# Moving the weight sums, the sums of squares and the closing normalisation of a hybrid decoder layer

## The chip, the cores and the metric

The program runs on one core of one Trainium2 chip. Its engines work side by side, each through its own queue in order: TensorE (PE in the profile; PEld is its loading of weights), VectorE (DVE), ScalarE (ACT) and GpSimd (POOL) compute; SyncE (SP) starts the transfers (DMA). The metric is device microseconds for one execution, lower is better; the number compared is the median over runs.

## What is computed

One decoder layer over 1024 tokens of width 1024, float32, with three sub-layers. Each is a root-mean-square norm, a function, another norm and an addition to the residual stream:

```
def rmsnorm(x, g):
    xf = x * rsqrt(mean(x * x, axis=-1) + 1e-6)
    return xf * g

h = rmsnorm(x, g_mix_pre)                       # 1 mixing: S5 state space + chunked gMLP
mix = concat([y_ssm(h), y_gmlp(h)]) @ w_out
x = x + rmsnorm(mix, g_mix_post)
h = rmsnorm(x, g_x_pre)                         # 2 cross-attention, 4 heads, 256 memory tokens
q, k, v = h @ w_q, mem_n @ w_k, mem_n @ w_v
x = x + rmsnorm((softmax(q k^T / 16) v) @ w_o, g_x_post)
h = rmsnorm(x, g_ffn_pre)                       # 3 gated convolutional FFN, d_ff 2816
a = causal_conv3(h @ w_up)
x = x + rmsnorm((a_val * gelu(a_gate)) @ w_down, g_ffn_post)
```

## The kernel before

**Layout.** Activations lie transposed: a tile holds 128 channels by 512 tokens. The tokens are two halves, h = 0 and 1, so a full activation is eight tiles per half. To keep float32 precision each operand is split into a high and a low part (a copy on ScalarE, a subtraction on VectorE or GpSimd), and each product is three matmuls (`mm3`, L227). Weights come through a stream (`Stream`, L64): SP loads a 128x512 raw tile, ScalarE makes the high part (L131), VectorE the low part (L134). PSUM has four banks "acc", three "sx" and one "st". The up and down projections use Strassen-like block products, for which sums of weight blocks are formed on GpSimd; for the down projection these are made beforehand by `s_sums` (L1342): for each of 11 blocks four loads, four sums (L1354), four stores to DRAM scratch "sd".

**Order.** The Python program gives a priority, and a scheduler that simulates the engines fixes the order of every queue before the launch. While `self.pinned` is true, the instructions passed through `pin` (L222) keep the program's order. Work beside the main products is written as generators that advance by one `yield` at each tick; `mm3` ticks twice for each product of eight blocks.

**Attention (L1048).** For each half the projection "o1" (L1094: eight products of 24 matmuls) makes the output of the mixers. `post(..., "q", ...)` (L712) then takes the statistics (L715), and for each of eight tiles loads a residual tile "rs" (L722, two buffers), multiplies (L723, VectorE), adds the residual (L724, GpSimd), stores x1d (L725), makes the high and the low part of the query input (L729, L730), squares (L709, ScalarE) and adds the square to a running sum (L710, GpSimd in this mode). The generator then passes `Q_STATS` = 3 ticks and calls `rms` (L738 through L273): matmuls against ones (L278) that sum over channels, and an inverse square root in small VectorE steps (L261 to L270). The result `qscale` enters the softmax as the scale of the exponentials (L1128). In the loop over six stages (L1163) stage i computes the query blocks of head i (`q_block`, two of 24 matmuls), the scores and softmax of head i-1 (`scores`), and the transposes (L1142) and weighted sums of head i-2. A step of `s_sums` is taken at most places of this loop, so it runs through both halves. The output projection "o2" follows; during half 0's the `post` of half 1 runs at its side, and during the attention of half 1 the `post2[0]` of half 0 (mode "f": sums of squares on VectorE). Attention's tiles "t" (11 buffers) hold queries, probabilities and transposes.

**End (L1442).** The last block product accumulates into four banks, first 256 columns of half 1 (quarter 0: 11 blocks by 4 banks by 3 matmuls of 256 columns), then the other 256 (quarter 1). Beside quarter 0 the generator `first_half` (L1497) sums the squares of half 0's eight tiles, and `finish` (L755) takes statistics, broadcasts them (L305, then a copy to SBUF, L308), multiplies (L766) and adds the residual (L767), and stores. In quarter 1 the order is pinned from the second bank on; after block `TAIL_R` = (1, 1) come the statistics of quarter 0, after `TAIL_B` = (1, 9) their broadcast, and its four pairs of tiles are finished (L774, L776) between the matmuls. After quarter 1 the same follows for its own columns.

Of the kernel before, what the change touches and what calls it, by code (L numbers as in the profile page):

```python
# [43 lines left out]
Q_STATS = 3  # L44
TAIL_R = (1, 1)
TAIL_B = (1, 9)
# [9 lines left out]
SLOTS_2 = {"kv": 16, "t": 11, "rs": 2}  # L56
# [95 lines left out]
class Builder:  # L152
# [120 lines left out]
    def rms(self, acc, nt):  # L273

        nc = self.nc
        ps = self.bank("st")
        for i in range(nt):
            self.pin(nc.tensor.matmul(ps[:, i:i + 1], lhsT=acc[:, i * P:(i + 1) * P], rhs=self.ones[:, 0:1],  # L278
                                      start=True, stop=True))
        x = self.tiny([P, nt], "st_x", 2)  # L280
        self.pin(nc.vector.tensor_scalar(x, ps[:, :nt], 1.0 / D, EPS, ALU.mult, ALU.add))
        return self.rsqrt(x, [P, nt])
# [17 lines left out]
    def bcast(self, r, nt, tag="st"):  # L300

        nc = self.nc
        ps = self.bank("st")
        for i in range(nt):
            self.pin(nc.tensor.matmul(ps[:, i * P:(i + 1) * P], lhsT=r[:, i:i + 1].to_broadcast([P, P]),  # L305
                                      rhs=self.ident, start=True, stop=True))
        bc = self.slot(tag)
        nc.scalar.copy(bc[:, :nt * P], ps[:, :nt * P])  # L308
        return ps, bc
# [402 lines left out]
    def post(self, m, acc, gpost, res, h, mode, dst):  # L712
# [5 lines left out]
        outp = self.xg[h] = []  # L718
        for i in range(KT):
            x = m[i]  # L720
            rs = self.slot("rs")
            nc.sync.dma_start(rs, res(i, h))  # L722
# [9 lines left out]
            self.sumsq(x, acc2, i == 0, v if mode == "f" else g)  # L732
            yield
        if mode == "q":
            self.ready[h] = True
            for _ in range(Q_STATS):
                yield
# [17 lines left out]
    def finish(self, m, acc, h, x2d):  # L755

        nc, v, g = self.nc, self.nc.vector, self.nc.gpsimd
        res = []
        for i in range(KT):
            t = self.slot("rs")  # L760
            nc.sync.dma_start(t, x2d[i][h])
            res.append(t)
        r, bc = yield from self.stats(acc, 4)
        for i in range(KT):
            x = m[i]
            v.scalar_tensor_tensor(x, x, self.gain["g_ffn_post"][:, i:i + 1], bc, ALU.mult, ALU.mult)  # L766
            g.tensor_tensor(x, x, res[i], ALU.add)  # L767
            yield
            nc.sync.dma_start(self.out[P * i:P * i + P, HALF * h:HALF * h + HALF], x)
# [33 lines left out]
    def prepare(self, cp, dp):  # L803
# [78 lines left out]
        self.ready = [False, False]  # L882
        self.mix = {}
# [164 lines left out]
    def attention(self):  # L1048
# [41 lines left out]
        post = [None, None]  # L1090
        kv = self.side(kv_parts(), 1)
        for h in range(2):
            for b in range(8):
                proj(lambda k, hh: self.mix[k, hh], "o1", m1, sq1, b, h, (4, 5, 6, 7, 0, 1, 2, 3))  # L1094
            for k in range(8):
# [64 lines left out]
        s_job = self.s_sums()  # L1160
        for h in range(2):
            heads = lambda k, hh: oT[hh][k]
            for i in range(6):  # L1163
# [5 lines left out]
                if i == 1:  # L1169
                    self.drain(post[h])  # L1170
                if 1 <= i <= 4:
                    scores(h, i - 1)
                for j in range(2):
                    if i:
                        next(s_job, None)
                    if i < 4:
                        q_block(h, i, j)
                    if i >= 2:
                        turn(i - 2) if j == 0 else weigh(h, i - 2)
            self.xg[h] = []  # L1180
            if h == 0:
                self.side(post[1])
# [159 lines left out]
    def s_sums(self):  # L1342

        nc, g = self.nc, self.nc.gpsimd
        for k in range(11):
            t = {}
            for o in range(2):
                for j in range(2):
                    t[o, j] = self.slot("m")
# [92 lines left out]
    def down(self):  # L1442
# [74 lines left out]

        for k in range(11):
# [7 lines left out]
            next(job, None)  # L1526
        self.drain(job)
        st = {}
        for b in range(4):
            self.pinned = b > 0  # L1530
            for k in range(11):
                one(k, b, quarters[1])
                if (b, k) == TAIL_R:
                    st["r"] = self.rms(sq[1][:, quarters[0]], 2)
                if (b, k) == TAIL_B:
                    bc = self.bcast(st["r"], 2)[1]
# [87 lines left out]
```

## Time and profile before

| what | us |
|---|---|
| median of 3 runs (1373.46 to 1376.73) | 1373.87 |
| profiled execution, its own time | 1375.64 |
| its span, first to last instruction | 1373.8 |
| VectorE busy in the span | 1066.1 |
| GpSimd busy in the span | 694.6 |
| ScalarE busy in the span | 628.0 |

The difference between the own time and the span lies outside the instructions. Busy time of an engine that is not the bottleneck costs nothing by itself; what matters in each stretch is which wait ended last. Matmuls are pipelined, so one may last 0.4 us in the profile while the next starts 0.23 us after it. A bracket at the end of a timeline line gives the idle time before it and what ended it.

### The profile page before, as it was taken

The page shows a single profiled execution, that of the slowest core. Times are in us where ns is not written, and L with a number is a line of the kernel's source. Part 1 is how long each engine was busy: PE and PEld are TensorE (multiplying, and loading weights), DVE is VectorE, ACT ScalarE, POOL GpSimd, SP SyncE. Part 2 cuts the span into 40 slices and gives each one's busy share as a digit, 9 for nine tenths or more (in the row PEclk, how much of TensorE's full clock was granted, in tenths as well). Part 3 has the DMA queues.
Part 4 walks back from the last instruction along what each step waited for, and adds up shares of the span by engine and source line. Part 5 has one row for each costly group of instructions (what it writes and reads, how often), then busy time and mean ns, then how long its engine had stood idle before and what let it go on. Part 6 is the DMA issues. An engine that isn't in the chain of part 4 may idle for free. (4 is left out here: it accounts for less than half of the span.)

```text
span 1373.8 us, 19246 instructions
## 1 busy us (share of the span) xinstructions
PE 1275.9 (93%) x6352; PEld 1080.4 (79%) x6352; DVE 1066.1 (78%) x1619; ACT 628.0 (46%) x1172; POOL 694.6 (51%) x532
## 2 busy tenths in 40 slices
PE   9799898779998999769999999999999999999993
PEld 7689897678886888558887878888888888788883
DVE  7968799876377757796657978888899879966576
ACT  7223331246444445345544654555555554446340
POOL 1586355834258524860343838656565227822144
PEclk9899999899998999979999999999999999999996
DMA  9654326256348844772358566545454359755123
GB/s 319 185 143 134 93 73 182 85 148 192 93 125 263 299 134 125 266 245 85 83 163 282 161 209 229 180 149 161 146 182 140 107 198 383 233 159 175 56 79 136
DMA packets 150662, 233.58 MB, mean 170 GB/s; under 512 B 33697, under 2 KB 43041, under 8 KB 150561
## 3 DMA queue, kind: packets, MB, share of 16 engines
q1 hardware_dynamic: 150560, 232.34, 53.3%
q8 instruction: 50, 0.82, 0.3%
q14 instruction: 52, 0.42, 0.1%
HBM read 174.23 MB, written 53.85 MB: 166 GB/s over the span
## 5 line engine op out<-in xcount | busy, mean ns | idle before, releaser
L233 PE MATMUL acc<-b,w 128*128 128x512 f32 x2412 | 587.9, 397 | 11.4 <-DVE b L730 4.4
L233 PEld LDWEIGHTS acc<-b,w 128*128 128x128 f32 x2412 | 457.6, 191 | 110.2 <-DVE b L730 6.5
L134 DVE TENSOR_TENSOR w<-raw,w 128x512 fp32r<-128x512 f32 x206 | 203.1, 994 | 94.2 <-PE acc L233 64.6
L233 PE MATMUL sx<-b,w 128*128 128x512 f32 x921 | 222.6, 391 | 1.7 <-ACT T L1277 1.7
L233 PEld LDWEIGHTS sx<-b,w 128*128 128x128 f32 x921 | 174.0, 189 | 38.5 <-ACT T L1277 2.1
L131 ACT CAST w<-raw 128x512 fp32r<-128x512 f32 x228 | 141.4, 622 | 125.3 <-PE acc L233 72.1
L710 POOL TENSOR_TENSOR ac<-ac,sq 128x512 f32<-128x512 f32 x52 | 78.3, 1513 | 153.2 <-ACT sq L709 152.6
L233 PE MATMUL acc<-T,w 128*128 128x512 f32 x528 | 127.0, 389 | 0.0
L233 PEld LDWEIGHTS acc<-T,w 128*128 128x128 f32 x528 | 99.1, 188 | 20.5
L253 DVE TENSOR_TENSOR w<-b,w 128x512 fp32r<-128x512 f32 x64 | 67.4, 1065 | 23.7 <-PE st L233 8.6
L1400 POOL TENSOR_TENSOR f<-f,f 128x512 f32<-128x512 f32 x33 | 55.0, 1678 | 48.1 <-DMA f<-fd 35.5
L1354 POOL TENSOR_TENSOR m<-m,m 128x512 f32<-128x512 f32 x44 | 62.8, 1432 | 31.3 <-DMA m<-in_w_dk 22.3
L724 POOL TENSOR_TENSOR m<-m,rs 128x512 f32<-128x512 f32 x32 | 49.3, 1545 | 48.6 <-DMA rs<-x1d 18.9
L233 PE MATMUL sx<-T,w 128*128 128x512 f32 x264 | 66.5, 389 | 0.0
L253 DVE TENSOR_TENSOR b<-f,b 128x512 fp32r<-128x512 f32 x53 | 54.4, 1041 | 4.3 <-ACT b L252 4.0
L233 PEld LDWEIGHTS sx<-T,w 128*128 128x128 f32 x264 | 49.6, 188 | 10.3
L709 ACT ACTIVATE sq<-m 128x512 f32<-128x512 f32 x66 | 41.3, 630 | 30.6 <-POOL m L724 13.5
L1216 POOL TENSOR_TENSOR b<-b,m 128x512 f32<-128x512 f32 x22 | 32.5, 1478 | 44.7 <-ACT m L1215 44.2
L115 POOL TENSOR_TENSOR st<-st,b 128x512 f32<-128x512 f32 x20 | 26.6, 1328 | 52.5 <-DMA st<-in_w_up 29.4
L252 ACT CAST w<-b 128x512 fp32r<-128x512 f32 x64 | 39.5, 619 | 27.3 <-PE acc L233 16.9
L233 PE MATMUL acc<-w,b 128*128 128x256 f32 x384 | 50.9, 290 | 0.0
L252 ACT CAST b<-f 128x512 fp32r<-128x512 f32 x53 | 32.7, 619 | 38.4 <-DVE w L253 34.3
(345 smaller groups left out, 2278.9 us busy)
## 6 DMA issues: line engine op xcount, KB each, us to landing
raw<-in_w_up SPq DMA_DIRECT2D x68, 256.0 KB, 3.0
f<-fd SPq DMA_DIRECT2D x55, 256.0 KB, 4.6
m<-in_w_dk SPq DMA_DIRECT2D x44, 256.0 KB, 4.7
sd<-m SPq DMA_DIRECT2D x44, 256.0 KB, 3.8
b<-sd SPq DMA_DIRECT2D x44, 256.0 KB, 4.0
b<-in_w_up SPq DMA_DIRECT2D x40, 256.0 KB, 2.8
raw<-in_w_out SPq DMA_DIRECT2D x32, 256.0 KB, 2.7
raw<-in_w_q SPq DMA_DIRECT2D x32, 256.0 KB, 3.4
```

Of the source, the lines that this page charges most:

```text
L115: g.tensor_tensor(p["S4"], p["12"], p["S2"], ALU.subtract)
L131: nc.scalar.copy(hi[:, :w], t[:, :w])
L134: e.tensor_tensor(lo[:, :w], t[:, :w], hi[:, :w], ALU.subtract)
L233: self.pin(nc.tensor.matmul(ps, lhsT=x, rhs=y, start=first and i + j == 0, stop=last and i == n - 1 and j == 2, skip_group_check=go_on))
L252: self.nc.scalar.copy(hi, src)
L253: (e or self.nc.vector).tensor_tensor(lo, src, hi, ALU.subtract)
L709: nc.scalar.activation(sq, src, AF.Square)
L710: (e or nc.gpsimd).tensor_tensor(acc, acc, sq, ALU.add)
L724: g.tensor_tensor(x, x, rs, ALU.add)
L1216: nc.gpsimd.tensor_tensor(val, val, gate, ALU.mult)
L1354: g.tensor_tensor(t[to], t[x], t[y], op)
L1400: self.nc.gpsimd.tensor_tensor(s[to], s[x], s[y], ALU.subtract)
```

## The change

Five groups of edits:

1. `s_sums` starts before the first half's "o1" and takes one step after each of its eight products; the rest runs in the attention of half 0, and nothing is left for half 1. Its first four blocks load into "t" tiles in place of "m" tiles. "t" has 13 buffers in place of 11, and the two "rs" buffers of this part are gone.
2. `post` loads residual tiles up to four ahead, into "t" tiles (the FFN's `post2[1]` keeps "rs", one ahead), and adds all its squares on VectorE.
3. The statistics for the query scale are held back until the first scores: `q_done` is set in stage 1 after the query block (1, 0), and then the generator is drained. The scores come after the stage's first query block in place of before it.
4. At the end, the squares of half 0 are issued ahead of quarter 0; its statistics after block 8 of quarter 0; the broadcast and the eight tiles between the matmuls of quarter 1's first two banks. The tiles are multiplied by the broadcast in PSUM rather than by its copy; tiles 3 and 7 add the residual on VectorE. All of it is pinned.
5. The statistics of quarter 0 move from (1, 1) to (0, 7), their broadcast from (1, 9) to (1, 3), both into "sx" banks, and the whole of quarter 1 is pinned.

```diff
-Q_STATS = 3
-TAIL_R = (1, 1)
-TAIL_B = (1, 9)
+TAIL_R = (0, 7)
+TAIL_B = (1, 3)
+JOB_AT = (8,)
-SLOTS_2 = {"kv": 16, "t": 11, "rs": 2}
+SLOTS_2 = {"kv": 16, "t": 13}
...
-    def rms(self, acc, nt):
+    def rms(self, acc, nt, bank="st"):
-        ps = self.bank("st")
+        ps = self.bank(bank)
...
-    def bcast(self, r, nt, tag="st"):
+    def bcast(self, r, nt, tag="st", bank="st"):
-        ps = self.bank("st")
+        ps = self.bank(bank)
...
+        late = (mode, h) == ("f", 1)
+        held = []
         for i in range(KT):
             x = m[i]
-            rs = self.slot("rs")
-            nc.sync.dma_start(rs, res(i, h))
+            while len(held) < min(KT, i + (1 if late else 4)):
+                held.append(self.slot("rs" if late else "t"))
+                nc.sync.dma_start(held[-1], res(len(held) - 1, h))
+            rs = held[i]
...
-            self.sumsq(x, acc2, i == 0, v if mode == "f" else g)
+            self.sumsq(x, acc2, i == 0, v)
             yield
         if mode == "q":
             self.ready[h] = True
-            for _ in range(Q_STATS):
+            while not self.q_done[h]:
                 yield
...
-        r, bc = yield from self.stats(acc, 4)
+        r = self.rms(acc, 4)
+        yield
+        bc = self.bcast(r, 4)[0]
+        yield
         for i in range(KT):
             x = m[i]
-            v.scalar_tensor_tensor(x, x, self.gain["g_ffn_post"][:, i:i + 1], bc, ALU.mult, ALU.mult)
-            g.tensor_tensor(x, x, res[i], ALU.add)
+            self.pin(v.scalar_tensor_tensor(x, x, self.gain["g_ffn_post"][:, i:i + 1], bc, ALU.mult, ALU.mult))
+            e = v if i % 4 == 3 else g
+            self.pin(e.tensor_tensor(x, x, res[i], ALU.add))
+            nc.sync.dma_start(self.out[P * i:P * i + P, HALF * h:HALF * h + HALF], x)
             yield
-            nc.sync.dma_start(self.out[P * i:P * i + P, HALF * h:HALF * h + HALF], x)
...
+        s_job = self.s_sums()
         kv = self.side(kv_parts(), 1)
         for h in range(2):
             for b in range(8):
                 proj(lambda k, hh: self.mix[k, hh], "o1", m1, sq1, b, h, (4, 5, 6, 7, 0, 1, 2, 3))
+                if h == 0:
+                    next(s_job)
...
-        s_job = self.s_sums()
...
-                if i == 1:
-                    self.drain(post[h])
-                if 1 <= i <= 4:
-                    scores(h, i - 1)
                 for j in range(2):
                     if i:
                         next(s_job, None)
                     if i < 4:
                         q_block(h, i, j)
+                    if j == 0:
+                        if i == 1:
+                            self.q_done[h] = True
+                            self.drain(post[h])
+                        if 1 <= i <= 4:
+                            scores(h, i - 1)
                     if i >= 2:
                         turn(i - 2) if j == 0 else weigh(h, i - 2)
             self.xg[h] = []
             if h == 0:
+                self.drain(s_job)
                 self.side(post[1])
...
-                    t[o, j] = self.slot("m")
+                    t[o, j] = self.slot("t" if k < 4 else "m")
...
+        next(job)
+        next(job)
         for k in range(11):
...
-            next(job, None)
-        self.drain(job)
+            if k in JOB_AT:
+                next(job)
         st = {}
+        self.pinned = True
         for b in range(4):
-            self.pinned = b > 0
             for k in range(11):
                 one(k, b, quarters[1])
+                if k % 2 == 0 and b < 2:
+                    next(job, None)
                 if (b, k) == TAIL_R:
-                    st["r"] = self.rms(sq[1][:, quarters[0]], 2)
+                    st["r"] = self.rms(sq[1][:, quarters[0]], 2, "sx")
                 if (b, k) == TAIL_B:
-                    bc = self.bcast(st["r"], 2)[1]
+                    bc = self.bcast(st["r"], 2, "st", "sx")[1]
```

More of the change, by code (lines that the diff above doesn't have):

```diff
@@ L882, in prepare @@
         self.ready = [False, False]
+        self.q_done = [False, False]
         self.mix = {}
```

## The prediction, made before the changed kernel was run

> **What bounds the kernel.** The page first:
>
> ```profile
> span 1373.8 us, 19246 instructions
> PE 1275.9 (93%) x6352; PEld 1080.4 (79%) x6352; DVE 1066.1 (78%) x1619; ACT 628.0 (46%) x1172; POOL 694.6 (51%) x532
> ```
>
> TensorE is the limit, and the change takes no matmul away; only the roughly 98 us in which it stands, and what a lowered clock costs after a stop, can be won. So I looked by windows for stretches where its busy time falls short, with the clock and the weight sums' new place beside them (columns: the stretch, its length, busy time of PE, PEld, DVE, ACT, POOL with counts, clock, DMA share, GB/s):
>
> ```profile
> 340.00:381.00 41.00, 41.00 (x185) 33.99 (x183) 13.10 (x15) 17.47 (x31) 9.00 (x7) 1.00 0.35 96
> 409.00:440.00 31.00, 24.50 (x95) 20.00 (x96) 23.88 (x30) 15.15 (x27) 23.54 (x16) 0.83 0.77 241
> 545.00:625.00 80.00, 60.90 (x270) 47.49 (x270) 68.43 (x91) 31.86 (x66) 55.04 (x38) 0.89 0.74 246
> 1326.00:1361.00 35.00, 21.54 (x157) 20.97 (x156) 25.65 (x42) 5.98 (x16) 18.91 (x12) 0.80 0.36 121
> ```
>
> Three of them are holes: the starts of the attention of half 0 and half 1, and the end. All that TensorE waited for between 400 and 640 us (total, times, longest):
>
> ```profile
> PE st L278 <- POOL ac L710: 7.4, 2, 6.5
> PE sx L1142 <- ACT t L1128: 7.1, 1, 7.1
> PE sx L233 <- ACT t L252: 4.4, 3, 3.5
> PE acc L233 <- DVE b L730: 4.4, 3, 2.4
> PE sx L233 <- DVE t L253: 1.9, 3, 0.9
> PE acc L233 <- DVE w L134: 0.7, 1, 0.7
> PE st L305 <- DVE rs_y L270: 0.2, 1, 0.2
> ```
>
> That is 26.1 us: 7.2 at half 0 (6.5 and 0.7), 18.9 at half 1. TensorE's timeline adds the clock, against a full-speed block from the chain of work:
>
> ```profile
> 428.27 1.86 PE L278 MATMUL st<-ones,ac 128*128 128x1 f32 x8 [6.50 <-POOL ac L710]
> 429.99 11.89 PE L233 MATMUL acc<-b,w 128*128 128x512 f32 x39
> 615.88 6.99 PE L233 MATMUL acc<-b,w 128*128 128x512 f32 x21
> 756.18 5.44 PE sx L233 x24
> ```
>
> A matmul starts every 5.44/24 = 0.227 us. The 39 after the 6.50 us stop should take 8.8 and took 11.7 without the overlap of 0.2: 2.9 lost. The 21 after the stops around 611 lost 2.1. So half 0's hole is worth 7.2 + 2.9 = 10.1 and half 1's 18.9 + 2.1 = 21.0.
>
> **Half 0 (groups 2 and 3).** GpSimd's timeline and the tile "ac" (min/median/max ns) show why the sums come late:
>
> ```profile
> 410.04 1.33 POOL L724 TENSOR_TENSOR m<-m,rs 128x512 f32<-128x512 f32 x1 [1.64 <-DMA rs<-in_xT]
> 418.99 1.29 POOL L724 TENSOR_TENSOR m<-m,rs 128x512 f32<-128x512 f32 x1 [4.21 <-DMA rs<-in_xT]
> L710 POOL TENSOR_TENSOR ac<-ac,sq x52: 1265/1618/1749, 342.5 to 1323.2; 128x512 f32<-128x512 f32 x52
> L710 DVE TENSOR_TENSOR ac<-ac,sq x14: 678/692/1746, 606.7 to 741.0; 128x512 f32<-128x512 f32 x14
> ```
>
> With two residual buffers GpSimd waits for loads between its additions, then still has sums to do when TensorE reaches L278. Four loads ahead remove the first, VectorE's sums the second: seven of 1.62 leave GpSimd, seven of 0.69 to 1.75 go to VectorE, which was idle for 7.1 of the 31 us. And the statistics now stand three query blocks later, 3 x 5.44 = 16.3 us of matmuls behind the end of "o1". Behind them wait the exponentials, and behind these in ScalarE's queue the query splits; the next block covers them. I keep 0.5 for what is left: 9.6 won.
>
> **Half 1 (groups 1 to 3).** TensorE's last run of "o2", then VectorE and ScalarE:
>
> ```profile
> 529.06 20.62 PE L233 MATMUL acc<-b,w 128*128 128x512 f32 x88
> 529.97 9.55 DVE L723 SCALAR_TENSOR_TENSOR m<-m,gains,st 128x512 f32<-128x512 f32 x8 [2.35 <-ACT st L308]
> 562.40 1.01 DVE L730 SCALAR_TENSOR_TENSOR b<-m,gains,b 128x512 fp32r<-128x512 f32 x1 [2.77 <-ACT b L729]
> 522.25 0.16 DVE L263 TENSOR_TENSOR rs_t<-rs_y 128x4 f32<-128x4 f32 x1
> 575.24 1.21 DVE L263 TENSOR_TENSOR rs_t<-rs_y 128x4 f32<-128x4 f32 x1
> 583.14 0.56 ACT L1128 ACTIVATE t<-sx,mx,rs_y 128x256 f32<-128x256 f32 x1 [10.65 <-DVE mx L1124]
> 594.35 9.54 DVE L723 SCALAR_TENSOR_TENSOR m<-m,gains,st 128x512 f32<-128x512 f32 x8
> ```
>
> Eight multiplications L723 and then, for each tile, a weight split, L730 and now also a sum: 24 VectorE instructions. TensorE reaches these inputs at about 549.7 (the end of "o2"). In the trace the last L730 ended at 563.4, held by its load and by GpSimd's additions. Without both, L723 still ends near 539.5; GpSimd's eight additions (next fence: 1.545 each) run until 543 and the two tiles in that time take 3 x 1.75; the other six go at 3 x 0.7 us, so the last input comes near 558: I keep 3.5 us of waiting, against 4.4. The larger part hangs on the small steps: alone one takes 0.16 us, beside GpSimd's weight sums 1.21, so the query scale came late, ScalarE stood 10.65 us before an exponential with the query splits queued behind it, and later L723 x8 stood before the next reductions (7.1 and 4.4 in the waits). The weight sums are gone from here, but the same L723 x8 come, perhaps now before the scale, which itself starts one block later. I take 5.5 for that, between nothing and the 11.5 of before, and 2 for the clock: 11.0 left, **10.0 won**.
>
> **Group 1, the new place.**
>
> ```profile
> L1354 POOL TENSOR_TENSOR m<-m,m 128x512 f32<-128x512 f32 x44 | 62.8, 1432 | 31.3 <-DMA m<-in_w_dk 22.3 <-DMA sd<-m 4.5 <-DVE rs_t L269 1.9
> L724 POOL TENSOR_TENSOR m<-m,rs 128x512 f32<-128x512 f32 x32 | 49.3, 1545 | 48.6 <-DMA rs<-x1d 18.9 <-DVE m L723 16.2 <-DMA rs<-in_xT 11.4
> ```
>
> Four blocks bring 16 sums x 1.43 = 22.9 us to GpSimd, which had 9.0 of 41 us of work between 340 and 381, and 32 transfers of 256 KB, 8.4 MB: 205 GB/s on top of 96, more than the 246 of the hole at half 1. TensorE is busy throughout there, so nothing can be won. The sums of squares of "o1" queue behind the weight sums, and L278 behind the last of them; at worst that is a group of four, 5.7, with its loads' mean wait of 31.3/11 = 2.8, and the clock's 2.9: 11.4. But the fourth group is issued after the last square, and the third two products (10.9 us) before it. I take **2**, near the lower end. Placing four blocks in "t" costs nothing while no query exists; SP's queue takes the 32 issues between weight loads that have six tiles of lead.
>
> **Groups 4 and 5, the end.**
>
> ```profile
> 1310.22 8.79 PE L233 MATMUL acc<-f,w 128*128 128x256 f32 x72
> 1316.65 7.88 POOL L710 TENSOR_TENSOR ac<-ac,sq 128x512 f32<-128x512 f32 x5 [0.31 <-ACT sq L709]
> 1333.33 11.47 DVE L766 SCALAR_TENSOR_TENSOR m<-m,gains,st 128x512 f32<-128x512 f32 x8 [1.38 <-ACT st L308]
> 1334.15 12.98 POOL L767 TENSOR_TENSOR m<-m,rs 128x512 f32<-128x512 f32 x8 [9.62 <-DVE m L766]
> 1344.72 0.15 DVE L281 TENSOR_SCALAR st_x<-st 128x2 f32<-128x2 f32 x1
> 1348.86 1.19 PE L305 MATMUL st<-ident,rs_y 128*128 128x128 f32 x4 [11.94 <-DVE rs_y L270]
> 1361.09 0.61 PE L278 MATMUL st<-ones,ac 128*128 128x1 f32 x4 [0.94 <-DVE ac L1516]
> 1365.31 1.29 DVE L774 TENSOR_TENSOR m<-m,st 128x512 f32<-128x512 f32 x2 [1.45 <-ACT st L308]
> 1365.35 1.27 POOL L774 TENSOR_TENSOR m<-m,st 128x512 f32<-128x512 f32 x1 [8.72 <-ACT st L308]
> ```
>
> TensorE stands 11.94 us before quarter 0's broadcast, because VectorE does eight multiplications ahead of the 4.1 us of small steps (1344.72 to 1348.86). Now in the new order, at 8.79/72 = 0.122 us a matmul: quarter 0's 132 end at 1326.3. Half 0's statistics stand after 108 of them, at 1323.4, and wait for the sums until 1324.5; with this 1.1 and 1.0 for L278, quarter 1 starts at 1328.4; the small steps, at 4.1, are done by 1329.6 and the broadcast by 1330.6. Three multiplications follow on VectorE: 0.65 each if PSUM operands do as in the L774 that ran beside GpSimd at 1365 (1.29/2), 11.47/8 = 1.43 if as L766 now; I take 0.65, since the operand is of that kind. Quarter 0's statistics come 21 matmuls later, done at 1333.8; the small steps end near 1337.9, where TensorE has stood since 1336.4. Its broadcast ends at 1338.9, and 87 matmuls later, 10.6, it is 1349.5; the last square adds 1, so the closing L278 comes at 1350.5, for 1361.09: 10.6 won. VectorE's rest (five multiplications, two additions, four pair steps) is some 10 us and fits. At 1.43 it is 16, ends near 1354, and 7 are won. Pinned, any late link holds all behind it; I take **9.5**. Nothing later changes: the closing steps stay as they are.
>
> **Sum**, against the profiled execution's own 1375.64 (span 1373.8 and 1.8 around it): 9.6 + 10.0 + 9.5 - 2.0 = 27.1, so 1348.5. The median of the runs, 1373.87, lies 1.8 below that execution; I leave this to the range. The feed-forward part between is paced by TensorE and should only start earlier.
>
> **Rivals.** *VectorE takes over at half 1.* It is busy 68.4 of the 80 us, and seven sums are added. For it: the 1746 ns of the longest sum; against it: GpSimd loses the same seven and all weight sums there. Half 1 wins nothing: 9.6 + 9.5 - 2 = 17.1, 1358.5. The Trainium skill, "SBUF — State Buffer", section "Who interferes with whom", says that a VectorE instruction with two SBUF inputs and a GpSimd instruction reading SBUF exclude each other for a whole instruction; this speaks against squares summed on VectorE beside residual additions on GpSimd. By it all fourteen sums could take the longest 1.75 rather than the median 0.69, 14.8 us more, 7.4 at half 1: 1355.9. The trace agrees in the two lengths of L710 on VectorE, but its median says that most sums escape.
>
> *The end's pinned order stops TensorE twice* (at half 0's broadcast and at quarter 0's) for the old 12 us together: 9.6 + 10.0 - 2 = 17.6, 1358.0. Against it stands the working above.
>
> *Slower: "t" runs out.* Thirteen tiles serve what eleven and two did, but four are held for residuals while half 1's heads need ten at their peak (queries, probabilities, transposes: 2 + 4 + 4): fourteen. A query split then waits for a tile, its bank stays full, and TensorE loses a block, 5.44, and 2.9 of clock at each of four heads: 33.4; with nothing won at half 1, 1375.6 - 17.1 + 33.4 = 1391.9. It turns the sign from 17.1/4 = 4.3 us a head. Against it: residual tiles are freed every 1.5 us by GpSimd.
>
> *Everything goes*: 10.1 + 21.0 + 10.6 = 41.7, 1333.9. *The change does not do what it says*: the program gives only priorities; if the scheduler fills VectorE and TensorE in the old order, the waits stay, 1374.
>
> **Numbers.** Forecast 0.48 (its own range 1340 to 1357), VectorE 0.20, pinned order 0.08, "t" 0.10, everything 0.08, nothing 0.06. The range 1334 to 1366 leaves out "t", nothing, and half of everything: 0.20. About 0.3% is what a measurement of this kernel can tell from no change: faster 0.48 + 0.20 + 0.08 + 0.08 = 0.84, same 0.06, slower 0.10.
>
> **What would show it.** Right: no wait of L278 for GpSimd near 428; residual loads issued ahead of GpSimd's additions; no L1354 after 500; L1142 without its 7 us; L766 at 0.65 to 0.75 and the 11.94 below 3; the closing L278 near 1334. Wrong: L278 waiting near 381 for the sums (group 1), waits for "t" tiles on ScalarE or in SP's queue, L710 on VectorE at 1.7 with L730 still last near 563, or TensorE standing at both broadcasts of the end.

## The result and the profile after

The changed kernel takes 1355.43 us (median of 4 runs, 1352.88 to 1357.03) against 1375.23 (4 runs) on the same chip: ratio 0.9855, 95% interval 0.9831 to 0.9879. That is faster by 19.8 us; the forecast was 1348.5. The profiled execution is the fastest of the four, 1352.88, and its span is 23.1 us below that of before. The page's first lines:

```profile
span 1350.7 us, 19249 instructions
PE 1272.3 (94%) x6352; PEld 1081.4 (80%) x6352; DVE 1061.3 (79%) x1635; ACT 629.2 (47%) x1172; POOL 678.3 (50%) x516
```

TensorE's busy time is nearly what it was (1275.9), so most of the 23 us came out of its standing time. To see where, I divided both spans at marks that stand behind the same number of matmuls in both: the broadcast of half 0's first statistics (behind 2066; 389.11 before, 391.05 after), a place in half 0's "o2" (behind 2639; 515.74, 511.56), the broadcast of `post2[1]` (behind 3456; 709.09, 697.01), quarter 0's first matmul (behind 6056; 1310.22, 1295.16), and the closing L278 (1361.09, 1338.11).

The second mark needs care. In the changed kernel the statistics (L278) in half 0's "o2" stand there, at 511.56. In the kernel before they stand 20 matmuls later, at 520.28, behind 20 x 0.227 = 4.5 us more of work. So that instruction is not the same point in both. Some of the expectations below use it all the same: their 131.2 and 188.8 us for the halves of before are 126.6 and 193.4 between equal marks.

| stage | before | after | won | forecast |
|---|---|---|---|---|
| ahead | 389.11 | 391.05 | -1.9 | -2.0 |
| half 0 | 126.63 | 120.51 | **6.1** | **9.6** |
| half 1 | 193.35 | 185.45 | 7.9 | 10.0 |
| feed-forward | 601.13 | 598.15 | 3.0 | 0 |
| end | 50.87 | 42.95 | 7.9 | 9.5 |
| after the end | 12.71 | 12.59 | 0.1 | 0 |

Half 0 is furthest below its forecast. TensorE's waits of after between 400 and 640 us (total, times, longest) show what is left:

```profile
PE st L278 <- DVE mx L1136: 7.0, 1, 7.0
PE st L278 <- POOL ac L710: 5.2, 1, 5.2
PE sx L233 <- DVE t L253: 2.3, 1, 2.3
PE sx L1154 <- ACT t L1140: 1.0, 2, 0.5
PE acc L233 <- DVE w L134: 0.2, 1, 0.2
```

26.1 us of waiting became 15.7: 7.2 became 3.0 at half 0, and 18.9 became 12.7 at half 1. The 7.1 at the transposes (now L1154) and the 4.4 at the last query inputs are gone. Three new stops have come, one at half 0 and two at half 1; these two belong to `post2[0]`. In TensorE's timeline of after:

```profile
437.42 0.94 PE L278 MATMUL st<-ones,ac 128*128 128x1 f32 x8
455.11 3.19 PE L233 MATMUL sx<-kv,t 128*128 128x256 f32 x19 [2.27 <-DVE t L253]
558.23 1.87 PE L278 MATMUL st<-ones,ac 128*128 128x1 f32 x8 [5.19 <-POOL ac L710]
559.96 9.18 PE L233 MATMUL acc<-b,w 128*128 128x512 f32 x27
601.15 1.84 PE L278 MATMUL st<-ones,ac 128*128 128x1 f32 x8 [7.03 <-DVE mx L1136]
```

The query scale's statistics of half 0 (437.42) have no bracket left. In their place TensorE stands 2.27 us at 455.11, before the second head's scores, for the low part of a query split. Its high part stands in ScalarE's queue behind the exponentials, which run from 448.93 to 451.1:

```profile
453.55 0.58 ACT L252 CAST t<-acc 128x512 fp32r<-128x512 f32 x1
```

From 455.11 to 464.29 TensorE's granted clock is 0.81, which costs some 1.7 of these 9.2 us.

At half 1 TensorE stands 5.19 us before the sums of "o2". The 27 matmuls behind it take 9.0 us (559.96 to 568.97, granted clock 0.67) rather than 27 x 0.227 = 6.1: 2.9 more for the clock. At 601.15 it stands 7.03 for the closing statistics of `post2[0]`, and runs at 0.72 from 602.85 to 610.10, which costs some 2.0. With the 0.5 of L1154 it stands 12.7 us in this stage, where the kernel before stood 19.2: 6.5 of the 7.9 won are standing time.

What happens on VectorE between those stops, in its timeline of after:

```profile
572.10 9.51 DVE L727 SCALAR_TENSOR_TENSOR m<-m,gains,st 128x512 f32<-128x512 f32 x8
582.74 0.15 DVE L281 TENSOR_SCALAR st_x<-st 128x4 f32<-128x4 f32 x1
587.51 0.17 DVE L743 TENSOR_SCALAR rs_y<-rs_y 128x4 f32<-128x4 f32 x1
```

The statistics of the query scale are ready on TensorE at 576.3 (its L278 began at 575.48), but their first small step, L281, stands behind the eight multiplications of `post2[0]` and comes at 582.74; the scale (L743) is done at 587.7. ScalarE's first exponential follows at 588.42:

```profile
588.42 0.57 ACT L1140 ACTIVATE t<-sx,mx,rs_y 128x256 f32<-128x256 f32 x1 [2.19 <-DVE mx L1136]
```

The second half of `post2[0]` is late for a reason of its own. SP issues four of its residual loads behind weight loads, and GpSimd stands for them (one line of each timeline):

```profile
588.72 1.85 SPq L725 DMA_DIRECT2D t<-x1d  x4
```

```profile
591.70 1.29 POOL L728 TENSOR_TENSOR m<-m,t 128x512 f32<-128x512 f32 x1 [11.96 <-DMA t<-x1d]
```

The squares and sums of these tiles come last before 601.15. The wait's label names L1136, but "ac" itself was last written by a VectorE sum that began at 600.3.

Half 0 and the weight sums, in GpSimd's timeline of after:

```profile
325.80 9.79 POOL L1368 TENSOR_TENSOR t<-t,t 128x512 f32<-128x512 f32 x6
393.68 11.95 POOL L728 TENSOR_TENSOR m<-m,t 128x512 f32<-128x512 f32 x7 [3.50 <-DVE m L727]
483.91 5.41 POOL L1368 TENSOR_TENSOR m<-m,m 128x512 f32<-128x512 f32 x4 [4.45 <-DMA m<-in_w_dk]
```

Seven residual additions run in one stretch, without the DMA brackets of before. The weight sums (L1368, before L1354) begin at 325.80, before the "o1" of half 0, and the last four run from 483.91; none is left for half 1.

The end, on TensorE and then VectorE, of after:

```profile
1314.16 2.05 PE L305 MATMUL st<-ident,rs_y 128*128 128x128 f32 x8 [1.76 <-DVE rs_y L270]
1323.36 0.64 PE L305 MATMUL sx<-ident,rs_y 128*128 128x128 f32 x4
1338.11 0.98 PE L278 MATMUL st<-ones,ac 128*128 128x1 f32 x4 [3.69 <-DVE ac L1530]
```

```profile
1316.86 2.06 DVE L773 SCALAR_TENSOR_TENSOR m<-m,gains,st 128x512 f32<-128x512 f32 x3 [2.85 <-ACT st L308]
1328.48 1.77 DVE L782 TENSOR_TENSOR m<-m,st 128x512 f32<-128x512 f32 x1
1330.29 1.67 DVE L784 TENSOR_TENSOR m<-m,b 128x512 f32<-128x512 f32 x1
```

The 11.94 us before quarter 0's broadcast are gone (1323.36 has no bracket), the three multiplications take 2.06/3 = 0.69 each, and 1.76 stands at the first broadcast. New are the 3.69 before the closing statistics, and a low clock behind the 1.76: 0.51 from 1314.16 to 1320.40.

### The profile page after: what moved, and what is told of

Its sections match the earlier page's. It is cut to its first block, busy times and chain, and to the rows that moved or that the text cites. A ratio compares the mean times of both kernels' runs of the same rounds, so it can differ in the third digit from the quotient of the medians.

```text
span 1350.7 us, 19249 instructions
## 1 busy us (share of the span) xinstructions
PE 1272.3 (94%) x6352; PEld 1081.4 (80%) x6352; DVE 1061.3 (79%) x1635; ACT 629.2 (47%) x1172; POOL 678.3 (50%) x516
## 4 chain that ended last, share of the span: by engine, by line
PE 68%; DVE 17%; issue 5%; DMA 4%; POOL 3%; ACT 2%; SPq 1%; DVEq 0%; POOLq 0%; ACTq 0%
PE acc L233 45%; PE sx L233 18%; DVE w L134 3%; PE st L233 2%; DVE m L727 1%; DVE w L253 1%; DMA m<-in_xT 1%; PE st L305 1%; PE st L278 1%; DVE ac L710 1%; DVE b L253 1%; DMA x<-x 1%; POOL ac L710 1%; DVE x L597 1%; DMA k<-gd 1%
## 5 line engine op out<-in xcount | busy, mean ns | idle before, releaser
L233 PE MATMUL acc<-b,w 128*128 128x512 f32 x2412 | 580.2, 394 | 7.8 <-ACT m L1481 4.1
L131 ACT CAST w<-raw 128x512 fp32r<-128x512 f32 x228 | 141.3, 621 | 126.6 <-PE acc L233 59.4
L710 POOL TENSOR_TENSOR ac<-ac,sq 128x512 f32<-128x512 f32 x38 | 58.2, 1531 | 166.2 <-ACT sq L709 165.6
L728 POOL TENSOR_TENSOR m<-m,t 128x512 f32<-128x512 f32 x24 | 40.0, 1697 | 42.6 <-DVE m L727 29.5
L233 PE MATMUL acc<-w,b 128*128 128x256 f32 x384 | 50.9, 290 | 0.0
L134 POOL TENSOR_TENSOR w<-raw,w 128x512 fp32r<-128x512 f32 x22 | 30.1, 1369 | 39.1 <-ACT w L131 26.7
```

What stands on the lines that cost most here:

```text
L131: nc.scalar.copy(hi[:, :w], t[:, :w])
L134: e.tensor_tensor(lo[:, :w], t[:, :w], hi[:, :w], ALU.subtract)
L233: self.pin(nc.tensor.matmul(ps, lhsT=x, rhs=y, start=first and i + j == 0, stop=last and i == n - 1 and j == 2, skip_group_check=go_on))
L710: (e or nc.gpsimd).tensor_tensor(acc, acc, sq, ALU.add)
L728: g.tensor_tensor(x, x, rs, ALU.add)
```

## The experiments

All kernels are divided at the same marks, behind 2066, 2639, 3456 and 6056 matmuls and at the closing L278 of their profiled executions. In `tail_only` and `early_scale`, as in the kernel before, the L278 in half 0's "o2" stands 20 matmuls behind the second mark. Where a kernel has one time and no interval, it is that of this execution. `m_res`, `tail_ps`, `early_scale` and `sq_pool` ran on another chip than the other experiments; there the kernel before took 1370.28, in one run. The stages, in us ("first exp." is the first exponential of half 1, counted from the end of half 0):

| kernel | ahead | half 0 | half 1 | first exp. | feed-forward | end | span |
|---|---|---|---|---|---|---|---|
| before | 389.1 | 126.6 | 193.4 | 67.4 | 601.1 | 50.9 | 1373.8 |
| tail_only | 389.4 | 125.8 | 193.0 | 67.3 | 602.0 | 41.5 | 1363.8 |
| att_only | 393.0 | 121.4 | 184.4 | 76.2 | 599.4 | 50.9 | 1360.9 |
| **after** | 391.1 | 120.5 | 185.5 | 76.9 | 598.2 | 43.0 | 1350.7 |
| no_sums | 391.9 | 121.7 | 191.5 | 84.9 | 598.2 | 42.4 | 1358.2 |
| sq_own | 389.9 | 121.0 | 181.8 | 74.4 | 601.5 | 42.4 | 1349.3 |
| m_res | 392.3 | 120.7 | 183.7 | 82.1 | 598.3 | 41.5 | 1348.7 |
| tail_ps | 390.9 | 122.5 | 184.2 | 76.1 | 597.3 | 41.0 | 1348.2 |
| early_scale | 391.2 | 122.4 | 180.6 | 58.2 | 598.3 | 41.9 | 1346.9 |
| sq_pool | 394.4 | 126.5 | 186.1 | 77.8 | 600.9 | 41.6 | 1362.1 |
| **mix** | 392.9 | 121.3 | 177.7 | 60.7 | 597.4 | 42.4 | 1344.1 |
| mix_b | 393.1 | 119.3 | 180.6 | 67.3 | 600.4 | 41.9 | 1347.5 |
| mix_all | 392.7 | 120.7 | 183.9 | 68.5 | 601.0 | 40.1 | 1350.7 |
| mix_all_m | 391.0 | 123.3 | 181.5 | 75.0 | 600.5 | 40.1 | 1348.9 |

The table also says how far one execution can be read. Half 1 has the same edits in `after`, `att_only` and `tail_ps`: 184.2 to 185.5, mean 184.7. Half 0 lies between 119.3 and 123.3 (mean 121.2) in the nine kernels that leave it as the change made it, the stage ahead between 389.9 and 393.1 in the same nine. So one stage of two executions can differ by up to 4 us without an edit to it, and less than some 2 us from a mean says nothing. Against the means of `before` and `tail_only` (126.2 and 193.2) the change wins some 5 us at half 0 and 8.5 at half 1.

**The end alone, and the attention alone.** `tail_only` is the kernel before with groups 4 and 5; `att_only` is the changed kernel with these undone:

```diff
-TAIL_R = (0, 7)
-TAIL_B = (1, 3)
+TAIL_R = (1, 1)
+TAIL_B = (1, 9)
...
-        r = self.rms(acc, 4)
-        yield
-        bc = self.bcast(r, 4)[0]
-        yield
+        r, bc = yield from self.stats(acc, 4)
```

> Groups 4 and 5 alone on the kernel before. If the end's gain is its own (order of VectorE's work and broadcast in PSUM), the stretch from quarter 0's first matmul to the closing L278 falls from 50.9 us to about 43.0 as in the changed kernel, everything ahead of it stays, and the time is 8 us less, about 1367 (ratio 0.994). Rival: the end gained because the work ahead of it had finished earlier; then the stretch stays above 47.

> Groups 1 to 3 alone. If the groups add up, the stretch at the end stays at 50.9 us, half 0 (broadcast beside o1 to the statistics beside o2) takes 120.5 as in the changed kernel for 131.2 before, half 1 (from there to the broadcast at 697) 185.5 for 188.8, and the time is 12 to 15 us under the kernel before (ratio about 0.990). Rival: part of it is luck of the clock in the feed-forward part (3 us); then the sum is 12 and the feed-forward part takes 601 as before.

Measured: 1364.55 (ratio 0.9934, 0.9912 to 0.9955) and 1362.74 (0.9925, 0.9900 to 0.9951), against 1374.52. By medians the one wins 10.0 and the other 11.8, just under the 12 to 15 that were expected; together 21.8, where the whole change won 19.8. The parts add up within the intervals: the end does not give back what the attention wins. By stages the end is worth 50.87 - 41.54 = 9.3 alone and 7.9 in the whole.

**Group 1 undone.** `no_sums` puts the weight sums back into both attentions:

```diff
-        s_job = self.s_sums()
         kv = self.side(kv_parts(), 1)
...
-                if h == 0:
-                    next(s_job)
...
         self.post2 = [None, None]
+        s_job = self.s_sums()
```

> The changed kernel with the weight sums back in their old place. Theory: their GpSimd work slows VectorE's small steps and the query scale at half 1, so half 1 gets longer again (185.5 to 189 or more), and the 1.9 us lost ahead of half 0 come back. Rival: their place is indifferent at half 1, because the new waits there are others; then half 1 stays within 1 us of 185.5 and the whole is 1 to 2 us faster than the changed kernel.

Measured: 1360.92, and half 1 is 191.5, 6.8 above the 184.7; the other stages stay. The stage ahead is 391.9 with the sums no longer there, so its 1.9 us did not come back. VectorE's and GpSimd's timelines of this kernel show the mechanism:

```profile
587.50 0.15 DVE L281 TENSOR_SCALAR st_x<-st 128x4 f32<-128x4 f32 x1
590.90 1.25 DVE L261 TENSOR_SCALAR rs_y<-st_x 128x4 int32<-128x4 int32 x1
594.41 1.22 DVE L269 SCALAR_TENSOR_TENSOR rs_t<-rs_t,st_x 128x4 f32<-128x4 f32 x1
597.51 0.17 DVE L743 TENSOR_SCALAR rs_y<-rs_y 128x4 f32<-128x4 f32 x1
```

```profile
581.89 13.72 POOL L1365 TENSOR_TENSOR m<-m,m 128x512 f32<-128x512 f32 x8
```

While GpSimd adds weights the scale's chain takes 10 us from L281 to L743, where it took 4.8 in the changed kernel. So group 1 pays at half 1, as the prediction said, and by the same small steps.

**Group 3 undone in both halves.** `early_scale`:

```diff
-            while not self.q_done[h]:
+            for _ in range(3):
                 yield
...
+                if i == 1:
+                    self.drain(post[h])
+                if 1 <= i <= 4:
+                    scores(h, i - 1)
                 for j in range(2):
```

(and the block after `q_block` that did this is gone).

> Group 3 undone: the query scale after three ticks, the scores ahead of the stage's first query block. Theory: squares on VectorE and residuals four ahead are what removed half 0's wait; then L278 waits less than 2 us there and half 0 stays within 1.5 us of 120.5. Rival: only the later place hid it; then L278 waits 4 us or more for VectorE's sums and half 0 takes 125 or more.

Measured: 1348.89. L278 waits 4.25 us at half 0, as the rival said:

```profile
424.44 1.83 PE L278 MATMUL st<-ones,ac 128*128 128x1 f32 x8 [4.25 <-DVE ac L710]
```

But half 0 takes 122.4, 1.2 above the mean of 121.2 and inside the spread. (The 126.9 us up to its own L278, which would bear the rival out, hold 20 matmuls more.) That wait is the only one of half 0; the stop at the second head's scores, 2.1 to 3.9 us in the nine kernels with the late place, is gone.

Half 1 wins 184.7 - 180.6 = 4.1. Its VectorE timeline has the scale ahead of the multiplications:

```profile
566.69 0.17 DVE L743 TENSOR_SCALAR rs_y<-rs_y 128x4 f32<-128x4 f32 x1
578.62 11.61 DVE L727 SCALAR_TENSOR_TENSOR m<-m,gains,st 128x512 f32<-128x512 f32 x8 [1.44 <-ACT st L308]
```

So the late place of group 3 wins nothing at half 0 that these executions can tell, and costs at half 1. In half 0 it lets the sums finish, but the exponentials and the query splits behind them come late instead; in half 1 `post2[0]` brings eight multiplications, and the late place puts them ahead of the scale.

**Group 3 undone in half 1 only, whole and by parts.** `mix` undoes both parts there, `mix_b` only the place of the statistics:

```diff
-            while not self.q_done[h]:
+            n = 0
+            while not self.q_done[h] and (h == 0 or n < 3):
+                n += 1
                 yield
...
+                if h == 1 and i == 1:
+                    self.drain(post[h])
+                if h == 1 and 1 <= i <= 4:
+                    scores(h, i - 1)
...
-                    if j == 0:
+                    if h == 0 and j == 0:
```

(`mix_b` has the first hunk only.)

> The changed kernel, but half 1 takes its statistics for the query scale as before (three ticks after the last tile, the scores ahead of the stage's first query block); half 0 keeps the late place. Theory (the late scale wins 6.4 at half 0 and loses 9.4 at half 1, each independent of the other): half 0 near 120.5, half 1 near 176, end near 42.5, so the span near 1341 and the time near 1343, some 10 below the changed kernel's profiled 1352.88. Rival (the two halves hang together, because the sooner end of half 0 moves the residual loads and VectorE's additions of half 1 into the small steps): half 1 at 182 or more, time above 1349.

> As the kernel with the early scale in half 1 only, but half 1's scores stay behind the stage's first query block: of group 3's two parts in half 1 only the place of the statistics is undone. Theory (it is the statistics, which stand behind VectorE's eight multiplications of the second post): half 1 between 176 and 179. Rival (it is the place of the scores and with them of the exponentials): half 1 stays at 183 to 186.

Measured: `mix` 1347.17 (4 runs, 1345.55 to 1352.68; ratio 0.9812, 0.9782 to 0.9842, against 1373.75). Half 0 stays where it was (121.3) and half 1 falls to 177.7, 7.0 below the mean of 184.7; the span is 1344.1, not 1341. The theory's 6.4 and 9.4 came from the moved L278. That the halves are independent is not shown: with the same edits half 1 takes 180.6 in `early_scale`, 2.9 more. The interval of the ratio of `mix` overlaps that of the changed kernel, so that it beats this one rests on half 1's 7.0 us, not on the times alone. `mix_b` (1349.20) fell between the two expectations: 180.6. By this one execution of each the place of the statistics is worth 4.1 and that of the scores 2.9, the second not far from the spread. VectorE's timelines of `mix_b` and then of `mix` say how the second part works:

```profile
573.04 0.69 DVE L1137 TENSOR_REDUCE mx<-sx 128x2 f32<-128x512 f32 x1 [1.01 <-PE sx L233]
573.65 4.80 DVE L727 SCALAR_TENSOR_TENSOR m<-m,gains,st 128x512 f32<-128x512 f32 x4
578.37 1.24 DVE L1138 SCALAR_TENSOR_TENSOR mx<-mx,rs_y 128x2 f32<-128x2 f32 x1
```

```profile
573.43 0.69 DVE L1137 TENSOR_REDUCE mx<-sx 128x2 f32<-128x512 f32 x1 [2.38 <-PE sx L233]
574.16 0.16 DVE L1138 SCALAR_TENSOR_TENSOR mx<-mx,rs_y 128x2 f32<-128x2 f32 x1
```

With the scale known in both, four multiplications still slip between the reduction and the step that hands the maximum to ScalarE.

**Squares of the query posts back on GpSimd.** `sq_pool`:

```diff
-            self.sumsq(x, acc2, i == 0, v)
+            self.sumsq(x, acc2, i == 0, v if mode == "f" else g)
```

> The squares of the first two posts back on GpSimd, all else as changed. Theory: with the scale this late half 0 does not need VectorE's sums (within 1.5 us of 120.5), and at half 1 GpSimd's extra sums push o2's sums and L278's wait beyond 5.2, half 1 over 187. Rival: VectorE is the bound at half 1; then half 1 falls below 184.

Measured: 1363.84, and half 0 is 126.5: 5.3 above the mean, as long as in the kernel before, which I had not expected. Half 1 is 186.1, neither over 187 nor below 184, and its wait for "o2"'s sums is 2.51, not beyond 5.2. At half 0 TensorE does not wait for the sums themselves, but for VectorE's other work. The timelines of GpSimd, VectorE and TensorE:

```profile
412.37 3.40 POOL L710 TENSOR_TENSOR ac<-ac,sq 128x512 f32<-128x512 f32 x2
```

```profile
414.57 1.74 DVE L134 TENSOR_TENSOR w<-raw,w 128x512 fp32r<-128x512 f32 x1
```

```profile
416.37 28.64 PE L233 MATMUL acc<-b,w 128*128 128x512 f32 x118 [2.69 <-DVE w L134]
464.76 3.79 PE L233 MATMUL sx<-kv,t 128*128 128x256 f32 x19 [4.47 <-DVE t L253]
```

The first stop, 2.69, ends with a weight split that takes 1.74 us beside GpSimd's sums, 0.68 alone; it is the last of six VectorE steps in a row, from 406.08, of 1.74 to 1.78 each. The second, 4.47, is the stop that the changed kernel has at 455.11 with 2.27. There GpSimd runs weight sums, and what share the squares have in it is not shown.

**The two new stops, one by one.** `sq_own` gives the squares of half 0's "o2" tiles of their own among "t" instead of the two "sq" tiles shared with VectorE's sums; `m_res` holds the residual tiles of `post2[0]` in "m":

```diff
-            self.sumsq(t, sq[h], b == 0)
+            self.sumsq(t, sq[h], b == 0, tag="t" if (name, h) == ("o2", 0) else "sq")
```

```diff
-                held.append(self.slot("rs" if late else "t"))
+                held.append(self.slot("rs" if late else "m" if mode == "f" else "t"))
```

> The changed kernel, with the squares of half 0's o2 in t tiles of their own rather than in the two sq tiles that they share with half 1's post. Theory: L278 waits 5.2 us at half 1 because ScalarE's squares wait in order for a shared tile that VectorE's sum has not freed; then the wait falls below 1.5, its 2.9 of clock go too, and half 1 takes about 178 for 185.5. Rival: GpSimd's sums themselves are slow (1.5 each beside VectorE) or L278 simply stands too early; then the wait stays at 4 or more.

> The changed kernel with post2[0]'s residual tiles in free m tiles rather than in t (still four ahead). Theory: at half 1 the t tiles run out, so the loads of residuals five to eight are issued 26 us after the first four; the sums of squares and the second L278 (7.0 us of waiting, 2.6 of clock) hang on them. Then the loads come together, that wait falls below 2, and half 1 takes about 177 us for 185.5. Rival: VectorE's queue (eight multiplications of 9.5 us together, then splits and sums) is the cause, whatever the loads do; then the wait stays at 5 or more.

Measured: `sq_own` 1350.99; the wait for GpSimd's sums falls from 5.19 to 2.43, half 1 to 181.8, less than expected. So half of that wait is two squares in the same two buffers, which ScalarE fills in order for two readers. `m_res` 1350.64; SP now issues all eight loads by 557.03 and the 7.03 falls to 2.87:

```profile
594.08 1.02 PE L278 MATMUL st<-ones,ac 128*128 128x1 f32 x8 [2.87 <-DVE rs_y L270]
```

But half 1 is 183.7, within 1.0 of the mean. The first exponential moved from 76.9 to 82.1: with its loads there, the sums of `post2[0]` stand between the scale's small steps, and L743 comes at 594.63. The loads were a late link, but the scale stood right behind it.

**The closing wait.** `tail_ps` lets the VectorE pairs of quarter 0 read the broadcast in PSUM, not its copy:

```diff
-                    bc = self.bcast(st["r"], 2, "st", "sx")[1]
+                    ps, bc = self.bcast(st["r"], 2, "st", "sx")
...
-                    st["out"] = self.chain(*(self.finish_pair(mg[0][i], res[0][i], wide(bc), i, 1, 0, v)
+                    st["out"] = self.chain(*(self.finish_pair(mg[0][i], res[0][i], wide(ps), i, 1, 0, v)
```

> The changed kernel with quarter 0's broadcast read from PSUM by VectorE's two pairs at the end. Theory: the closing L278 waits 3.7 us because VectorE's pair steps meet GpSimd's (1.77 each for 0.65); with one SBUF tensor fewer the two multiplications take 0.65, the wait falls to about 1.4, and the stretch from quarter 0's first matmul to the closing L278 from 43.0 to about 40.7. Rival: the additions, still on two SBUF tensors, set the end; then the stretch stays above 42.

Measured: 1349.90; the closing wait falls from 3.69 to 1.96. VectorE's timeline of this kernel beside the 1.77 and 1.67 above:

```profile
1328.08 0.68 DVE L782 TENSOR_TENSOR m<-m,sx 128x512 f32<-128x512 f32 x1
1328.79 1.08 DVE L784 TENSOR_TENSOR m<-m,b 128x512 f32<-128x512 f32 x1
```

The three kernels with this edit have an end of 40.1 to 41.0, the nine others with the new end 41.5 to 43.0: 1.6 apart by their means. The spread of the nine goes with the clock behind the first broadcast. The same stop of 1.75 to 1.76 us stands before it in all of them, and the 15 matmuls behind it take 3.55 us in the changed kernel, but 2.04 in `early_scale` (granted clock 1.00), here in turn:

```profile
1315.86 3.55 PE L233 MATMUL acc<-f,w 128*128 128x256 f32 x15
```

```profile
1312.33 2.04 PE L233 MATMUL acc<-f,w 128*128 128x256 f32 x15
```

Of the nine, the five that take some 2.04 there have an end of 41.5 to 41.9, the three that take 2.52 to 2.68 one of 42.4, and the changed kernel one of 43.0.

**All gains together.** `mix_all` is `mix` with `tail_ps` and `sq_own`; `mix_all_m` adds `m_res`. No edit is new. (The tiles of their own go to the squares of half 0's "o2", which GpSimd adds, as in `sq_own`; the expectation names VectorE's squares.)

> The kernel with the early scale in half 1 only, and two more edits: quarter 1's VectorE steps at the end read the broadcast in PSUM, and VectorE's squares of half 0's second post get tiles of their own among 't'. If the gains add: half 0 near 120.5, half 1 near 174 (2 of the 3.7 that its own tiles gave, since the wait for GpSimd's sums was already shorter with the early scale), end near 41, time near 1339 to 1341. If the tiles of their own collide with the query splits that now come earlier: half 1 at 178 or more and no gain over the kernel without them.

> As the last, and the residual tiles of half 1's second post are held in 'm' tiles, so that their eight loads need not wait for 't' tiles. Theory (with the early scale the loads are no longer what comes last at half 1): within 2 of the last, 1338 to 1342. Rival (the loads are still the last link there): half 1 shorter by 3 to 5.

Measured: 1352.97 (0.9852, 0.9826 to 0.9878) and 1350.64 (0.9833, 0.9807 to 0.9860). The gains do not add. The end keeps its part (40.1), but half 1 goes from the 177.7 of `mix` to 183.9 and 181.5, which is what the expectation of `mix_all` named for tiles that collide. VectorE's timeline of `mix_all` shows another order:

```profile
575.00 0.68 DVE L1137 TENSOR_REDUCE mx<-sx 128x2 f32<-128x512 f32 x1
575.60 4.05 DVE L727 SCALAR_TENSOR_TENSOR m<-m,gains,st 128x512 f32<-128x512 f32 x6
579.58 0.68 DVE L1137 TENSOR_REDUCE mx<-sx 128x2 f32<-128x512 f32 x1
580.18 0.68 DVE L134 TENSOR_TENSOR w<-raw,w 128x512 fp32r<-128x512 f32 x1
580.78 0.15 DVE L1138 SCALAR_TENSOR_TENSOR mx<-mx,rs_y 128x2 f32<-128x2 f32 x1
```

The scale was known at 563.6, but six multiplications stand between the first reduction and its L1138. In `mix` that step came at once, and the six stood before the second reduction's (581.51). So with two edits that do not touch this order in the program the scheduler filled VectorE's queue otherwise. Part of the loss is also a longer stop at the query statistics (6.35 us, 4.99 in `mix`); what share each has was not tried. `mix_all_m` is 2.5 us below `mix_all` at half 1, which is near what one execution can tell; whether the loads' place wins it stays open.

## Why the prediction was right, and where it was wrong

The sign, the three places and the range were right; the sum was 27.1, and the profiled executions differ by 22.8 (1375.64 to 1352.88), the medians by 19.8. Part of that nearness is luck: the three places fall 3.5 + 2.1 + 1.6 = 7.2 us short of their forecast, and the feed-forward part gives 3.0 that the change, as far as the trace shows, did not cause.

**Half 0, the step that failed.** 9.6 forecast, 6.1 measured (some 5 by the means). What the prediction set out to remove is gone: GpSimd's additions run without DMA brackets, the sums are on VectorE, and L278 does not wait. What failed is its sentence on the exponentials and the query splits behind them, "the next block covers them", with 0.5 kept for all that is left. The next block does not cover them: TensorE stands 2.27 us for a query split and 3.0 in the whole stage, and the lowered clock behind it takes some 1.7. The experiments also part the two groups, which the prediction did not. Without group 3 (`early_scale`, 122.4) 4.2 of the 6.1 stay; without VectorE's squares (`sq_pool`, 126.5) nothing does. So the squares on VectorE carry this gain, and the late place adds nothing that can be told. The prediction named the sums' own lateness; `sq_pool` shows that VectorE's weight splits, slowed beside GpSimd's sums, are a part of it.

**Half 1, near the forecast by other terms.** 10.0 forecast, 7.9 measured (8.5 by the means). The prediction saw the danger of group 3 ("the same L723 x8 come, perhaps now before the scale, which itself starts one block later") and priced what stays at 5.5 us, "between nothing and the 11.5 of before". The late place costs 4.1 (`early_scale`) to 7.0 (`mix`) in this half, so that price was about right; without group 3 the other two groups win 193.35 - 180.60 = 12.75 there, more than the 10.0 of the sum. The reason is the order of VectorE's queue. With the first exponential half 1 goes from 177.7 at 60.7 (`mix`) over 180.6 at 67.3 (`mix_b`) and 185.5 at 76.9 to 191.5 at 84.9 (`no_sums`). This is a correspondence among four kernels, and no law: the kernel before takes 193.4 at 67.4, with other waits, `early_scale` 180.6 at 58.2, and `m_res`, with its loads in time, 183.7 at 82.1. What speaks for a cause is that the edits which move the scale move both.

Two smaller terms were misplaced. The 3.5 us for the last query input did not come: no wait for L734 (before L730) is left. In its place TensorE stops 5.19 us for GpSimd's "o2" sums, and loses 2.9 to the clock, in part because VectorE's sums now share the two "sq" tiles (2.43 are left in `sq_own`); the prediction costed those sums by their time on VectorE and not by their buffers. And it looked for a shortage of "t" as a lost block at each head, where the shortage shows as late residual loads: the 11.96 us on GpSimd. In all TensorE stands 12.7 us there, where the prediction kept 3.5 + 5.5 = 9.0.

**Group 1.** Its 2.0 us at the new place are neither shown nor refuted: the stage ahead is 1.9 longer, but as long in `no_sums`, where the sums have their old place. The L278 near 381, which the prediction named as the sign, has no wait. Its gain at half 1, 6.8, is shown.

**The end, right with a smaller size.** 9.5 forecast, 7.9 measured. The multiplications take 0.69 (forecast 0.65), and quarter 0's broadcast does not wait. Two terms were too small. The prediction put the clock behind the first broadcast's stop at nothing; where it stays up the same end takes 41.5 to 41.9, some 9 us won, and in the changed kernel 42.95. And it said of VectorE's rest that it "is some 10 us and fits": it took 13.6 (1323.14 to 1336.75), since beside GpSimd's pairs a step took 1.63 to 1.77, so the last square is late by 3.69 rather than 1.0.

**Feed-forward, 3.0 not forecast.** Not the change, as far as the trace shows: in TensorE's timelines, of before and then of after, the same place in the code runs at two granted clocks, 0.76 and 1.00.

```profile
796.63 7.35 PE L233 MATMUL acc<-b,w 128*128 128x512 f32 x24 [2.33 <-ACT t L1277]
803.82 5.60 PE L233 MATMUL sx<-b,w 128*128 128x512 f32 x24
```

```profile
782.36 5.76 PE L233 MATMUL acc<-b,w 128*128 128x512 f32 x24 [2.26 <-ACT t L1291]
787.95 5.60 PE L233 MATMUL sx<-b,w 128*128 128x512 f32 x24
```

A second such place is 23 matmuls at 742.74 of before, in 7.07 us (0.76), which take 5.50 in the changed kernel at 730.10 (1.00); there the stop ahead was 1.72 before and 0.75 after. The two make 1.6 + 1.6 = 3.2 us. Over all kernels the stage lies between 597.3 and 602.0.

**The rivals.** VectorE did not take over as a matter of load: it is busy 59.4 of the 80 us from 545 (68.4 before). Half 1 won 7.9 us, where this rival has nothing; what VectorE costs there comes by the order of its queue. On the rule in the Trainium skill, "SBUF — State Buffer", section "Who interferes with whom": the trace agrees, with L782 at 1.77 us on two SBUF inputs and 0.68 with one in PSUM, both beside GpSimd's pair steps. The price worked out from it, all fourteen sums at 1.75, did not come: between 505 and 640 us the fourteen take 13.0 us on VectorE, 0.93 each. "t" did not stop a head, the pinned order did not stop TensorE twice, and the scheduler did follow the program.

## What to carry to other kernels

Where a short chain of small steps releases another engine, ask what bulk work the in-order queue puts ahead of it, and ask it for each pass of the loop: the same later place changed nothing that could be told in one half, and cost 4 to 7 us in the half where a second normalisation runs beside it. Compare stages between marks that stand behind the same number of matmuls: an instruction of the same name can move with an edit, here by 4.5 us, and then one stage seems to win what the other did. Moving work to an idle engine is costed by its buffers too, here two tiles filled in order for two readers. Where a scheduler fills the queues, a gain measured for one edit holds for that order only: of three edits that each helped alone, two took back 6 of the 7 us that the third won at half 1.

## What the runs showed of the hardware

I had not expected that equal stops cost so differently. One of 2.33 us lowered TensorE's granted clock to 0.76 (24 matmuls in 7.35 us against 5.60), and one of 2.26 us at the same place of the code did not (1.00, 5.76). Before the first broadcast of the end twelve kernels have the same stop of 1.75 to 1.76 us; the 15 matmuls behind it take 2.03 or 2.04 us in seven of them, 2.52 to 2.68 in four, and 3.55 in the changed kernel. The Trainium skill, "TensorE: Matmul & The Clock Gate", Part 1, has a free-running window of about 3.4 us behind this; that one gap pays and an equal one does not would fit it, but no run here shows the window. Some 1.6 us for each such place is what a stage of this kernel can differ by without a change to it.
